# Diagonal of x·yᵀ with softmax: 32 KB runs in 4 MB halves, a last half cut into pieces, and the output moved to ACT's queue

## The chip, the cores and the metric

The kernel runs on one core of one Trainium2 chip. The metric is device time in microseconds (us). The kernel before was run again beside every experiment on the same chip, and its medians there lie between 333.78 and 334.00 us.

Words used throughout: a *dot* is one VectorE instruction that multiplies 128 rows of x by 128 rows of y, 512 numbers each, and sums every row. A *run* is what one packet moves, consecutive bytes of one partition. A *half* is 16 rows per partition, 4 MB of x and 4 MB of y; there are 16, numbered 0 to 15. A load *lands* when its completion is signalled. SP and ACT are the two engines whose queues issue loads here; ACT (ScalarE) also does the exp, and GpSimd the all-reduces over the partitions.

## The reference

```python
B, N, D = 8, 4096, 512            # x, y: float32, standard normal
gram = np.matmul(x, y.transpose(0, 2, 1))
diag = np.diagonal(gram, axis1=1, axis2=2)      # only these 8 x 4096 dots are needed
diag = diag - diag.max(axis=-1, keepdims=True)
exp = np.exp(diag)
return (exp / exp.sum(axis=-1, keepdims=True)).astype(np.float32)
```

The kernel must read 134.2 MB and write 0.13 MB.

## The kernel before

Each of 32 tiles is 8 rows per partition, 2 MB for each input. A batch is four tiles; after the fourth comes its softmax. The parts that matter, cut:

```python
io = ctx.enter_context(tc.tile_pool(name="io", bufs=3))
...
for i in range(n_tiles):                                   # 32 tiles, KR = 8
    x_tile = io.tile([P, KR, D], f32, tag="xt")
    y_tile = io.tile([P, KR, D], f32, tag="yt")
    nc.sync.dma_start(out=x_tile, in_=...)                 # SP queue
    nc.scalar.dma_start(out=y_tile, in_=...)               # ACT queue
    scratch = work.tile([P, D], f32, tag="scratch")        # one per tile
    for k in range(KR):
        nc.vector.scalar_tensor_tensor(
            out=scratch, in0=x_tile[:, k, :], scalar=1.0, in1=y_tile[:, k, :],
            op0=mult, op1=mult, accum_out=diag_sbuf[:, i*KR+k : i*KR+k+1])
    if (i + 1) % tiles_per_batch == 0:
        softmax_batch(b)       # max, all-reduce, exp on ACT, all-reduce, scale, output on SP
```

The order of instructions on each engine is set by the compiler, not by the program text alone.

## Time and profile before

| | us |
|---|---|
| timed, median of 4 runs | 334.00 (333.77 to 334.09) |
| span of the profile | 332.0 |
| last load lands | 321.04 |
| last dot done, maximum begins | 326.93 |
| output issued | 329.31 |

Four lines of the page of the kernel before: busy share of VectorE (DVE) and of the DMA engines in 40 equal slices, in tenths; what they moved; and the group of the dots (count, total busy us, mean ns of one, idle time before them and what ended most of it).

```profile
DVE  0355676543089811898038860588407973089834
...
DMA  8999999999999999999999999999999999999920
GB/s 322 426 438 424 432 423 428 426 427 428 428 436 426 428 422 432 416 426 427 427 432 430 418 432 422 438 377 433 422 431 436 414 431 421 438 393 418 428 127 2
...
L87 DVE SCALAR_TENSOR_TENSOR scratch<-x_tile,y_tile 128x512 f32<-128x512 f32 x256 | 176.9, 691 | 140.0 <-DMA x_tile<-in_x_dram 88.2
```

DMA is busy everywhere but at the ends: loads bound the kernel, and VectorE waits for them. So only three stretches can shrink: the time that the loads themselves take, the dots after the last landing, and the softmax and output after those. The tail, in the timeline of the kernel before (start us, us, engine, line, what, and in brackets the idle time before it and its releaser):

```profile
321.06 0.69 DVE L87 SCALAR_TENSOR_TENSOR scratch<-x_tile,y_tile 128x512 f32<-128x512 f32 x1 [4.96 <-DMA x_tile<-in_x_dram]
321.68 0.08 DVE L87 DVE_READ_ACCUMULATOR scratch<-x_tile,y_tile 128x1 f32 x1
321.80 0.69 DVE L87 SCALAR_TENSOR_TENSOR scratch<-x_tile,y_tile 128x512 f32<-128x512 f32 x1
...
326.93 0.19 DVE L52 TENSOR_REDUCE mxp<-diag_sbuf 128x1 f32<-128x32 f32 x1
...
329.31 0.40 SPq L73 DMA_DIRECT2D out_dram<-result_sbuf  x1
```

Eight dots follow the last landing. They start 0.73 us apart (321.06, 321.80). No load is left by then: the DMA share is 0.00 while they run.

### The profile page before, as it was taken

The page shows a single profiled execution, that of the slowest core. Times are in us where ns is not written, and L with a number is a line of the kernel's source. Part 1 is how long each engine was busy: PE and PEld are TensorE (multiplying, and loading weights), DVE is VectorE, ACT ScalarE, POOL GpSimd, SP SyncE. Part 2 cuts the span into 40 slices and gives each one's busy share as a digit, 9 for nine tenths or more (in the row PEclk, how much of TensorE's full clock was granted, in tenths as well). Part 3 has the DMA queues.
Part 4 walks back from the last instruction along what each step waited for, and adds up shares of the span by engine and source line. Part 5 has one row for each costly group of instructions (what it writes and reads, how often), then busy time and mean ns, then how long its engine had stood idle before and what let it go on. Part 6 is the DMA issues. An engine that isn't in the chain of part 4 may idle for free.

```text
span 332.0 us, 802 instructions
## 1 busy us (share of the span) xinstructions
DVE 183.0 (55%) x544; ACT 4.6 (1%) x17; POOL 6.1 (2%) x20
## 2 busy tenths in 40 slices
DVE  0355676543089811898038860588407973089834
ACT  0000100000000000000000000000000000000000
POOL 0000000000000000000000000000000000000000
DMA  8999999999999999999999999999999999999920
GB/s 322 426 438 424 432 423 428 426 427 428 428 436 426 428 422 432 416 426 427 427 432 430 418 432 422 438 377 433 422 431 436 414 431 421 438 393 418 428 127 2
DMA packets 13446, 134.40 MB, mean 405 GB/s; under 512 B 5248, under 2 KB 5248, under 8 KB 5248
## 3 DMA queue, kind: packets, MB, share of 16 engines
q1 hardware_dynamic: 8832, 67.24, 48.7%
q10 hardware_dynamic: 4608, 67.11, 47.3%
q14 instruction: 6, 0.05, 0.0%
HBM read 134.22 MB, written 0.13 MB: 405 GB/s over the span
## 4 chain that ended last, share of the span: by engine, by line
DMA 69%; DVE 25%; issue 2%; SPq 1%; POOL 1%; ACTq 0%; POOLq 0%; DVEq 0%
DMA x_tile<-in_x_dram 53%; DVE scratch L87 24%; DMA y_tile<-in_y_dram 17%; SPq L73 1%; POOL mx L54 1%; DVE result_sbuf L69 1%; DVE mxp L52 0%; ACTq L82 0%; DVE recip L68 0%; POOLq L124 0%; DVE neg_mx L56 0%; DVEq L69 0%; POOLq L54 0%; SPq L79 0%; DVEq L87 0%
## 5 line engine op out<-in xcount | busy, mean ns | idle before, releaser
L87 DVE SCALAR_TENSOR_TENSOR scratch<-x_tile,y_tile 128x512 f32<-128x512 f32 x256 | 176.9, 691 | 140.0 <-DMA x_tile<-in_x_dram 88.2
L87 DVE DVE_READ_ACCUMULATOR scratch<-x_tile,y_tile 128x1 f32 x256 | 20.8, 81 | 0.0
L54 POOL PARTITION_ALL_REDUCE mx<-mxp x8 | 2.8, 350 | 316.6 <-DVE mxp L52 316.6
L60 ACT ACTIVATE result_sbuf<-diag_sbuf,neg_mx 128x32 f32<-128x32 f32 x8 | 2.6, 321 | 284.5 <-DVE neg_mx L56 284.5
L56 DVE TENSOR_SCALAR neg_mx<-mx 128x1 f32<-128x1 f32 x8 | 1.2, 153 | 4.3 <-POOL mx L54 4.3
L66 POOL PARTITION_ALL_REDUCE ssum<-sump x8 | 3.1, 383 | 5.8 <-ACT result_sbuf L60 5.8
L69 DVE TENSOR_SCALAR result_sbuf<-result_sbuf,recip 128x32 f32<-128x32 f32 x8 | 1.9, 241 | 0.8
L60 ACT ACT_TABLE_LOAD x1 | 1.3, 1283 | 39.1 <-DVE scratch L87 39.1
L68 DVE RECIPROCAL recip<-ssum 128x1 f32<-128x1 f32 x8 | 1.3, 157 | 1.0 <-POOL ssum L66 1.0
L52 DVE TENSOR_REDUCE mxp<-diag_sbuf 128x1 f32<-128x32 f32 x8 | 1.5, 186 | 0.3
L60 ACT ACTIVATION_READ_ACCUMULATOR result_sbuf<-diag_sbuf,neg_mx 128x1 f32 x8 | 1.5, 186 | 0.0
L113 POOL MEMSET const-float32-0.0<- 128x1 f32 x1 | 0.1, 99 | 0.2 <-issue 0.2
L113 POOL MEMSET const-bfloat16-1.0<- 128x1 bf16 x1 | 0.1, 101 | 0.0
L113 POOL MEMSET const-uint8-127<- 128x1 uint8 x1 | 0.1, 101 | 0.0
L113 POOL MEMSET const-float32-1.0<- 128x1 f32 x1 | 0.1, 98 | 0.0
## 6 DMA issues: line engine op xcount, KB each, us to landing
y_tile<-in_y_dram ACTq DMA_DIRECT2D x32, 2048.0 KB, 13.8
x_tile<-in_x_dram SPq DMA_DIRECT2D x32, 2048.0 KB, 23.5
out_dram<-result_sbuf SPq DMA_DIRECT2D x8, 16.0 KB, 17.1
```

Of the source, the lines that this page charges most:

```text
L52: nc.vector.tensor_reduce(out=mxp, in_=db, axis=mybir.AxisListType.X, op=mybir.AluOpType.max)
L54: nc.gpsimd.partition_all_reduce(out_ap=mx, in_ap=mxp, channels=P, reduce_op=bass_isa.ReduceOp.max)
L56: nc.vector.tensor_single_scalar(out=neg_mx, in_=mx, scalar=-1.0, op=mybir.AluOpType.mult)
L60: nc.scalar.activation(out=exp_b, in_=db, func=mybir.ActivationFunctionType.Exp, bias=neg_mx, scale=1.0, accum_out=sump,)
L66: nc.gpsimd.partition_all_reduce(out_ap=ssum, in_ap=sump, channels=P, reduce_op=bass_isa.ReduceOp.add)
L68: nc.vector.reciprocal(out=recip, in_=ssum)
L69: nc.vector.tensor_single_scalar(out=exp_b, in_=exp_b, scalar=recip, op=mybir.AluOpType.mult)
L73: nc.sync.dma_start(out=dst_b, in_=res_b)
L87: nc.vector.scalar_tensor_tensor(out=scratch, in0=x_tile[:, k, :], scalar=1.0, in1=y_tile[:, k, :], op0=mybir.AluOpType.mult, op1=mybir.Al ...
L113: nc = _bacc.Bacc("TRN2", target_bir_lowering=False, num_devices=1)
```

## The change

Its intent: longer runs in HBM (32 KB instead of 16), fewer and larger loads, one straight 128-byte run per partition for the output, and a last half in pieces so that little work is left after the last byte. The diff also moves the output from SP's queue to ACT's and writes each product over x instead of to a scratch tile. The core of the diff, cut and with two comments added; the rest is renaming, and the softmax is the same but for its output.

```diff
-    KR = 8
+    R = N // P          # 32 consecutive rows per partition and batch
+    H = R // 2          # a half: 16 rows, 4 MB for each input
+    xv = x.rearrange("b (p r) d -> b p r d", p=P)
...
+        for n in parts:
+            nc.sync.dma_start(out=xt[:, o : o + n, :], in_=xv[b, :, r0 + o : r0 + o + n, :])
+            nc.scalar.dma_start(out=yt[:, o : o + n, :], in_=yv[b, :, r0 + o : r0 + o + n, :])
...
-                out=scratch,
-                in0=x_tile[:, k, :],
+                out=xt[:, k, :],
+                in0=xt[:, k, :],
...
-        nc.sync.dma_start(out=dst_b, in_=res_b)     # 512 packets of 32 bytes
+        nc.scalar.dma_start(out=ov[b], in_=rb)      # 128 packets of 128 bytes
...
+            parts = [8, 4, 2, 1, 1] if last else [H]
+            xt, yt = load(b, h * H, parts)
+            dots(b, h * H, xt, yt)
+        softmax(b)
```

More of the change, by code (lines that the diff above doesn't have):

```diff
@@ L22 @@
     B, N, D = x.shape
-    assert y.shape == (B, N, D)
-    assert out.shape == (B, N)
     P = nc.NUM_PARTITIONS
-    total = B * N
-    n_chunks = total // P
-    cpb = N // P
-    KR = 8
-    n_tiles = n_chunks // KR
-    tiles_per_batch = N // (P * KR)
-    assert tiles_per_batch * B == n_tiles
-    x_flat = x.flatten_outer_dims()
-    y_flat = y.flatten_outer_dims()
-    out_flat = out.flatten()
+    R = N // P
+    H = R // 2
+    xv = x.rearrange("b (p r) d -> b p r d", p=P)
+    yv = y.rearrange("b (p r) d -> b p r d", p=P)
@@ L41 @@
+    ov = out.rearrange("b (p r) -> b p r", p=P)
     io = ctx.enter_context(tc.tile_pool(name="io", bufs=3))
-    work = ctx.enter_context(tc.tile_pool(name="work", bufs=2))
     persist = ctx.enter_context(tc.tile_pool(name="persist", bufs=1))
     sm = ctx.enter_context(tc.tile_pool(name="sm", bufs=2))
-    diag_sbuf = persist.tile([P, n_chunks], f32)
-    result_sbuf = persist.tile([P, n_chunks], f32)
-    def softmax_batch(b):
-        db = diag_sbuf[:, cpb * b : cpb * (b + 1)]
-        mxp = sm.tile([P, 1], f32, tag="mxp")
-        nc.vector.tensor_reduce(out=mxp, in_=db, axis=mybir.AxisListType.X, op=mybir.AluOpType.max)
-        mx = sm.tile([P, 1], f32, tag="mx")
-        nc.gpsimd.partition_all_reduce(out_ap=mx, in_ap=mxp, channels=P, reduce_op=bass_isa.ReduceOp.max)
-        neg_mx = sm.tile([P, 1], f32, tag="nmx")
-        nc.vector.tensor_single_scalar(out=neg_mx, in_=mx, scalar=-1.0, op=mybir.AluOpType.mult)
-        exp_b = result_sbuf[:, cpb * b : cpb * (b + 1)]
-        sump = sm.tile([P, 1], f32, tag="sump")
-        nc.scalar.activation(
-            out=exp_b, in_=db,
-            func=mybir.ActivationFunctionType.Exp,
-            bias=neg_mx, scale=1.0, accum_out=sump,
-        )
-        ssum = sm.tile([P, 1], f32, tag="ssum")
-        nc.gpsimd.partition_all_reduce(out_ap=ssum, in_ap=sump, channels=P, reduce_op=bass_isa.ReduceOp.add)
-        recip = sm.tile([P, 1], f32, tag="recip")
-        nc.vector.reciprocal(out=recip, in_=ssum)
-        nc.vector.tensor_single_scalar(out=exp_b, in_=exp_b, scalar=recip, op=mybir.AluOpType.mult)
-        res_b = result_sbuf.rearrange("p (i kr) -> p i kr", kr=KR)[:, tiles_per_batch * b : tiles_per_batch * (b + 1), :]
-        dst_b = out_flat[b * N : (b + 1) * N].rearrange("(i p kr) -> p i kr", p=P, kr=KR)
-        nc.sync.dma_start(out=dst_b, in_=res_b)
@@ L75 @@
-    for i in range(n_tiles):
-        r0 = i * P * KR
-        x_tile = io.tile([P, KR, D], f32, tag="xt")
-        y_tile = io.tile([P, KR, D], f32, tag="yt")
-        nc.sync.dma_start(
-            out=x_tile, in_=x_flat[r0 : r0 + P * KR, :].rearrange("(p k) d -> p k d", p=P)
-        )
-        nc.scalar.dma_start(
-            out=y_tile, in_=y_flat[r0 : r0 + P * KR, :].rearrange("(p k) d -> p k d", p=P)
-        )
-        scratch = work.tile([P, D], f32, tag="scratch")
-        for k in range(KR):
+    diag = persist.tile([P, B * R], f32, name="diag")
@@ new lines, with load, dots @@
+    res = persist.tile([P, B * R], f32, name="res")
+    def load(b, r0, parts):
+        xt = io.tile([P, H, D], f32, tag="xt", name="xt")
+        yt = io.tile([P, H, D], f32, tag="yt", name="yt")
+        o = 0
+        for n in parts:
+            nc.sync.dma_start(out=xt[:, o : o + n, :], in_=xv[b, :, r0 + o : r0 + o + n, :])
+            nc.scalar.dma_start(out=yt[:, o : o + n, :], in_=yv[b, :, r0 + o : r0 + o + n, :])
+            o += n
+        return xt, yt
+    def dots(b, r0, xt, yt):
+        for k in range(H):
+            c = b * R + r0 + k
@@ L87, with softmax @@
             nc.vector.scalar_tensor_tensor(
-                out=scratch,
-                in0=x_tile[:, k, :],
+                out=xt[:, k, :],
+                in0=xt[:, k, :],
                 scalar=1.0,
-                in1=y_tile[:, k, :],
+                in1=yt[:, k, :],
                 op0=mybir.AluOpType.mult,
                 op1=mybir.AluOpType.mult,
-                accum_out=diag_sbuf[:, i * KR + k : i * KR + k + 1],
+                accum_out=diag[:, c : c + 1],
             )
-        if (i + 1) % tiles_per_batch == 0:
-            b = (i + 1) // tiles_per_batch - 1
-            softmax_batch(b)
+    def softmax(b):
+        db = diag[:, b * R : (b + 1) * R]
+        rb = res[:, b * R : (b + 1) * R]
+        mxp = sm.tile([P, 1], f32, tag="mxp", name="mxp")
+        nc.vector.tensor_reduce(out=mxp, in_=db, axis=mybir.AxisListType.X, op=mybir.AluOpType.max)
+        mx = sm.tile([P, 1], f32, tag="mx", name="mx")
+        nc.gpsimd.partition_all_reduce(out_ap=mx, in_ap=mxp, channels=P, reduce_op=bass_isa.ReduceOp.max)
+        nmx = sm.tile([P, 1], f32, tag="nmx", name="nmx")
+        nc.vector.tensor_single_scalar(out=nmx, in_=mx, scalar=-1.0, op=mybir.AluOpType.mult)
+        sump = sm.tile([P, 1], f32, tag="sump", name="sump")
+        nc.scalar.activation(
+            out=rb, in_=db, func=mybir.ActivationFunctionType.Exp,
+            bias=nmx, scale=1.0, accum_out=sump,
+        )
+        ssum = sm.tile([P, 1], f32, tag="ssum", name="ssum")
+        nc.gpsimd.partition_all_reduce(out_ap=ssum, in_ap=sump, channels=P, reduce_op=bass_isa.ReduceOp.add)
+        rc = sm.tile([P, 1], f32, tag="rc", name="rc")
+        nc.vector.reciprocal(out=rc, in_=ssum)
+        nc.vector.tensor_single_scalar(out=rb, in_=rb, scalar=rc, op=mybir.AluOpType.mult)
+        nc.scalar.dma_start(out=ov[b], in_=rb)
@@ L102 @@
+    for b in range(B):
+        for h in range(2):
+            last = b == B - 1 and h == 1
+            parts = [8, 4, 2, 1, 1] if last else [H]
+            xt, yt = load(b, h * H, parts)
+            dots(b, h * H, xt, yt)
+        softmax(b)
 _INS = ['x', 'y']
```

## The prediction

> **What bounds the kernel now.** Loads. The page's DMA row is at 9 tenths in every slice but the first and the last two, and moves some 428 GB/s; VectorE is busy 55%. In the trace's packet records nearly every 16 KB packet takes 611 ns on its engine, so 8192 of them on 16 engines are 312.8 us; they actually run from 1.7 to 319.6 us. The Trainium skill ("DMA: Bandwidth & Descriptors", Measured) gives 425 GB/s for a single core's 16 MB transfer, the same rate; so the bytes are at their ceiling, and the change moves the same bytes. Only what stands before the first packet (1.7 us), the roughly 5 us lost between packets, and the tail can shrink.
>
> **The tail (timeline).** The last x tile lands at 321.04; eight dot products of 0.733 us each follow (5.87 us), VectorE ends them at 326.9, and maximum, two all-reduces, exp, sum, scaling and the output DMA take 5.1 us more to 332.0. The timed median is 1.9 us over this span.
>
> **What the change does.**
> - Bigger descriptors (32 KB): 8 KB instruction packets took 307 ns and 16 KB 611, so some 3 ns are fixed; halving their number is worth 0.5 us or so.
> - Outputs: 32-byte packets fall from 4096 to 1024 of 128 bytes. They took 7 to 9 ns each; estimate 1 to 1.5 us saved over 16 engines.
> - Dropped scratch (product in place): the same instruction, nothing.
> - Output on ACT instead of SP: SP no longer stands behind the result (80 us of such waits on SP's queue). But DMA was never starved by them, because y filled in; it only removes the skew (x was up to 15 us behind y). x and y should now land together. Three 4 MB buffers keep over 8 us queued at all times (period 19.6 us, VectorE 11.7 us per half), so nothing starves.
> - First half lands at about 23 us instead of 13: harmless, VectorE catches up.
> - Tail: the last row pair is one 0.73 us dot product, but VectorE is then not idle. The half before it, 16 dots (11.7 us), starts 19.6 us before the last byte; 32 dots need 23.5 us. So VectorE ends about 3.9 us after the last landing (plus 0.3 for batch 6's reciprocal and scaling), not 0.73. Gain over 5.87: about 1.7 us, not 5.
>
> Sum: 332.0 - 1.7 (tail) - 1.3 (DMA) = 329.0 span; timed about 331.
>
> **Prediction: 331.0 us**, 80% between 328.0 and 334.5. Faster by over 2%: 0.07; within: 0.89; slower: 0.04.
>
> **What would show it.** The DMA row still near 428 GB/s; last load landing near 319.5; at that time VectorE still working on the 8-row or 4-row piece, without a gap from the start of the second-last half (16 dots) to the end; no idle time before the 1-row pieces' dots; x and y landing within about 1 us of each other throughout; span minus last landing about 9 us, before 11.
>
> **What would make it wrong.**
> - The instruction order is the compiler's. There seem to be 8 DMA semaphores in rotation (each load waits for the DMA eight before). If ACT gets the five y pieces before batch 6's exp, exp waits for the 8-row piece, the reciprocal for exp, and VectorE stalls: 5 to 11 us slower.
> - 32 KB runs at a 64 KB pitch could be read more slowly from HBM. The skill (same page, "Latency and other measured facts") shows such losses at far larger pitches of 512 KB and up; no run here shows it.
> - If packet stalls vanish (1 us at 216 and at 296 us of this trace), 327 is possible.
> - Skew left at the end lengthens the tail, since VectorE then gets both halves closer together.

## More of the kernel before

Most experiments ran on one chip; e10, e11 and e12 ran on another, where the kernel before took 333.88 us against 333.78 and 333.81. Differences between runs of separate sessions are therefore good to some 0.2 us.

The *lag* is the time by which the last of the DMA engines ends a load after the middle one.

## The result, and the profile after

The change took **331.92 us** (331.86 to 332.06, 4 runs) against 334.00: ratio 0.9939, 95% interval 0.9925 to 0.9953. Ratios here are the mean time of one kernel's fast runs over that of the other's fast runs of the same rounds, so not quite the ratio of the medians. The verdict is "same" at the 2% mark; a small gain is clear of noise.

| us | before | after | difference |
|---|---|---|---|
| last load lands | 321.04 | 318.36 | -2.7 |
| from there to the start of the maximum | 5.9 | 7.0 | +1.1 |
| from there to the end of the span | 5.1 | 4.7 | -0.4 |
| span | 332.0 | 330.0 | -2.0 |

The loads gained more than the whole kernel did, and the tail, which the pieces were to shorten, got *longer*. The same lines of the page of the change:

```profile
DVE  0029093470920561910878290660388465191995
...
DMA  8999999999999999999999999999999999999900
GB/s 318 445 445 445 409 426 433 445 445 409 423 441 445 441 405 429 439 445 429 413 431 445 445 418 417 439 441 445 409 427 441 441 433 410 443 417 423 396 37 3
...
L51 DVE SCALAR_TENSOR_TENSOR xt<-xt,yt 128x512 f32<-128x512 f32 x256 | 158.1, 687 | 151.8 <-DMA yt<-in_y_dram 151.8
```

Two things stand out. All of VectorE's large waits (151.8 us) are now for y, none for x. And the 256 dots keep VectorE busy for 158 us instead of 177, though one still takes about 690 ns: they overlap more. The tail in the change's timeline:

```profile
305.56 6.70 ACTq L44 DMA_DIRECT2D yt<-in_y_dram  x4
305.63 0.69 DVE L51 SCALAR_TENSOR_TENSOR xt<-xt,yt 128x512 f32<-128x512 f32 x1 [5.82 <-DMA yt<-in_y_dram]
306.25 0.69 DVE L51 SCALAR_TENSOR_TENSOR xt<-xt,yt 128x512 f32<-128x512 f32 x1
...
324.62 0.69 DVE L51 SCALAR_TENSOR_TENSOR xt<-xt,yt 128x512 f32<-128x512 f32 x1
325.35 0.19 DVE L65 TENSOR_REDUCE mxp<-diag 128x1 f32<-128x32 f32 x1
...
327.75 0.35 ACTq L80 DMA_DIRECT2D out_dram<-res  x1
```

Half 14 became complete only at 305.5, when its y landed; its x had landed at 288.7. From then on VectorE does 32 dots without a pause, 0.613 us apart (305.63, 306.25), which is 19.6 us, while the last byte lands only 12.8 us after half 14. VectorE therefore ends 7.0 us after the last landing, working off a backlog. The size of the last piece no longer matters.

Why y trails shows on ACT's own queue. In the change's timeline of ACT (ACTq is its sequencer, which issues the loads), around the first softmax:

```profile
52.84 0.32 ACT L71 ACTIVATE res<-diag,nmx 128x32 f32<-128x32 f32 x1 [49.45 <-DVE nmx L69]
52.85 0.34 ACTq L44 DMA_DIRECT2D yt<-in_y_dram  x1
53.07 0.19 ACT L71 ACTIVATION_READ_ACCUMULATOR res<-diag,nmx 128x1 f32 x1
63.94 0.35 ACTq L80 DMA_DIRECT2D out_dram<-res  x1
64.33 0.44 ACTq L44 DMA_DIRECT2D yt<-in_y_dram  x1
```

The y load issued at 52.85 had its buffer free since 32.5, and the x load of the same half went out on SP at 32.54. It stood behind the exp, which needed the dots of the next half. The y load at 64.33 stood behind the output; its x partner went out at 51.98. The trace has this order, exp, y, output, y, for each of the batches 0 to 5.

The trace's packet records showed a third thing. Each load ends on each of 16 DMA engines with a 4-byte packet, so one can see when each engine finished. (The records do not name the engine; that it is one and the same is read from there being one late packet per load.) In the last y load of the change, the middle engine was done at 314.19 and the last one at 317.91: **one DMA engine ran 3.7 us behind the rest**, and the landing is set by the last. In the last x load of the kernel before that lag was 1.8 us.

### The profile page after: what moved, and what is told of

Read it like the earlier page. It is cut to its first block, busy times and chain, and to the rows that moved or that the text cites. A ratio compares the mean times of both kernels' runs of the same rounds, so it can differ in the third digit from the quotient of the medians.

```text
span 330.0 us, 732 instructions
## 1 busy us (share of the span) xinstructions
DVE 163.9 (50%) x544; ACT 4.6 (1%) x17; POOL 6.1 (2%) x20
## 4 chain that ended last, share of the span: by engine, by line
DMA 72%; DVE 24%; issue 2%; POOL 1%; ACTq 0%; POOLq 0%; DVEq 0%; ACT 0%
DMA yt<-in_y_dram 72%; DVE xt L51 23%; POOL mx L67 1%; DVE mxp L65 0%; DVE nmx L69 0%; ACTq L44 0%; DVE res L79 0%; POOLq L114 0%; POOL ssum L76 0%; DVE rc L78 0%; ACTq L80 0%; ACT res L71 0%; DVEq L51 0%; POOLq L67 0%; DVEq L79 0%
## 5 line engine op out<-in xcount | busy, mean ns | idle before, releaser
L51 DVE SCALAR_TENSOR_TENSOR xt<-xt,yt 128x512 f32<-128x512 f32 x256 | 158.1, 687 | 151.8 <-DMA yt<-in_y_dram 151.8
L51 DVE DVE_READ_ACCUMULATOR xt<-xt,yt 128x1 f32 x256 | 21.1, 82 | 0.0
L71 ACT ACTIVATE res<-diag,nmx 128x32 f32<-128x32 f32 x8 | 2.6, 321 | 320.0 <-DVE nmx L69 320.0
L78 DVE RECIPROCAL rc<-ssum 128x1 f32<-128x1 f32 x8 | 1.3, 163 | 6.7 <-POOL ssum L76 6.7
L69 DVE TENSOR_SCALAR nmx<-mx 128x1 f32<-128x1 f32 x8 | 1.2, 154 | 4.3 <-POOL mx L67 4.3
L79 DVE TENSOR_SCALAR res<-res,rc 128x32 f32<-128x32 f32 x8 | 1.9, 241 | 0.7
L65 DVE TENSOR_REDUCE mxp<-diag 128x1 f32<-128x32 f32 x8 | 1.5, 186 | 0.3
L71 ACT ACTIVATION_READ_ACCUMULATOR res<-diag,nmx 128x1 f32 x8 | 1.5, 186 | 0.0
```

The costliest lines, as they stand in the source:

```text
L51: nc.vector.scalar_tensor_tensor(out=xt[:, k, :], in0=xt[:, k, :], scalar=1.0, in1=yt[:, k, :], op0=mybir.AluOpType.mult, op1=mybir.AluOpT ...
L65: nc.vector.tensor_reduce(out=mxp, in_=db, axis=mybir.AxisListType.X, op=mybir.AluOpType.max)
L69: nc.vector.tensor_single_scalar(out=nmx, in_=mx, scalar=-1.0, op=mybir.AluOpType.mult)
L71: nc.scalar.activation(out=rb, in_=db, func=mybir.ActivationFunctionType.Exp, bias=nmx, scale=1.0, accum_out=sump,)
L78: nc.vector.reciprocal(out=rc, in_=ssum)
L79: nc.vector.tensor_single_scalar(out=rb, in_=rb, scalar=rc, op=mybir.AluOpType.mult)
```

## The experiments

Eleven kernels ran; all gave the reference's result. Theory A: the skew between x and y, made by ACT's order, lengthens the tail. Rivals: the queue count, or the pieces themselves. Further theories concern the in-place product, the run length, the outputs and the lagging engine. All numbers, the decisive columns from timeline and landings (blank: not used). At the 2% mark e1 and e6 are faster than the kernel before, e8 and e10 unclear, and all others the same:

| run | timed us | ratio to before | half 14 complete | last load lands | maximum begins |
|---|---|---|---|---|---|
| the change | 331.92 | 0.9939 | 305.5 | 318.4 | 325.4 |
| e1 y on SP | 325.50 | 0.9752 | 298.4 | 318.2 | 319.1 |
| e5 e1 with self-wait | 328.31 | 0.9834 | 298.4 | 318.3 | 321.9 |
| e9 y early | 332.31 | 0.9951 | 306.0 | 318.3 | 326.0 |
| e10 in step, two queues | 327.57 | 0.9813 | 298.7 | 318.4 | 319.2 |
| e4 no pieces | 334.88 | 1.0032 | 308.4 | 318.1 | 328.2 |
| e12 e1 without pieces | 334.25 | 1.0012 | 298.4 | 317.8 | 327.8 |
| e6 e1, few instructions | 322.98 | 0.9671 | 295.7 | 315.7 | 316.5 |
| e11 e1, more instructions | 329.36 | 0.9869 | 301.3 | 322.1 | 322.9 |
| e7 e1 with 16 KB runs | 328.15 | 0.9827 | | 320.7 | |
| e8 e1 with 32-byte outputs | 327.20 | 0.9803 | | 318.2 | 319.1 |
| e3 before, in place | 332.88 | 0.9970 | | 320.8 | 325.8 |

### e1: y on SP

```diff
-            nc.scalar.dma_start(out=yt[:, o : o + n, :], ...)
+            nc.sync.dma_start(out=yt[:, o : o + n, :], ...)
```

> The change with the y loads moved from the ACT queue to the SP queue, nothing else. Theory A (y's loads stand behind exp and the output on ACT, so y trails x by up to 20 us, the last two halves become complete only 12.8 us apart, and VectorE's 32 dot products of 0.613 us = 19.6 us end 7.0 us after the last landing): x and y of a half now land within 1 us of each other, the second-last half is complete about 19 us before the last landing, VectorE ends 1 to 2 us after the last landing, time 326.5 to 328 us against 331.9 for the change. Rival B (the tail is set by the pieces and the landing of the last one, skew does not matter): time within 1 us of 331.9. Rival C (one queue feeds the DMA engines less well than two): DMA rate below 428 GB/s, last landing later than 320.

Measured: 325.50 us, 6.4 us under the change (difference of the medians) and 1.0 below the range expected. The last landing hardly moved (318.23), so the loads run no worse from one queue. Half 14 was complete 19.9 us before it, and VectorE all but kept up. The end of e1's timeline:

```profile
317.05 0.69 DVE L51 SCALAR_TENSOR_TENSOR xt<-xt,yt 128x512 f32<-128x512 f32 x1
317.67 0.08 DVE L51 DVE_READ_ACCUMULATOR xt<-xt,yt 128x1 f32 x1
318.33 0.69 DVE L51 SCALAR_TENSOR_TENSOR xt<-xt,yt 128x512 f32<-128x512 f32 x1 [0.58 <-DMA yt<-in_y_dram]
318.94 0.08 DVE L51 DVE_READ_ACCUMULATOR xt<-xt,yt 128x1 f32 x1
319.06 0.19 DVE L65 TENSOR_REDUCE mxp<-diag 128x1 f32<-128x32 f32 x1
```

Now the last dot waits 0.58 us for the last row: the tail is one dot long, as the change had intended. Theory A holds and rivals B and C fall; whether a single queue as such was the cause is left to e9 and e10. One slip in the expectation: with a single queue x and y of a half do not land within 1 us of each other but take turns about 10 us apart; what matters is that whole halves become complete evenly.

### e9 and e10: in step on two queues

e9 leaves y on ACT and moves the loads up in the program.

```diff
+    tiles = {j: load_half(j) for j in range(3)}
+    for j in range(2 * B):
+        ...
+        dots(b, h * H, xt, yt)
+        if j + 3 < 2 * B:
+            tiles[j + 3] = load_half(j + 3)
+        if h == 1:
+            softmax(b)
```

> The change with y left on the ACT queue, but each half's loads are written in the program right after the dots that free its buffer, ahead of that batch's softmax, so that on ACT most y loads no longer stand behind exp and the output. It tells skew from queue. Theory A (skew between x and y is what lengthened the tail): x and y land within 2 us of each other, second-last half complete 18 us or more before the last landing, VectorE ends 1 to 2 us after it, time 325 to 327. Rival (a single queue as such made e1_y_on_sp fast): time stays near 331.9.

Measured: 332.31 us, and the skew was still there (half 14 complete at 306.0): the edit missed its aim, so this run tells nothing between skew and queue. In its trace the first batch's output went out on ACT only at 102.8, since VectorE reached that batch's reciprocal late; the y load behind it left at 103.2, its x partner at 91.7. After that, x and y of a half are issued within 2.1 us of each other, up to half 14, and yet from half 6 to half 14 y lands 19 to 31 us after x. The likely reading: x, with less waiting in its queue, lands first, and then has to wait for buffers that only y can free. The delay, once there, did not heal; no run separates the first late load from the 2 us that y loses behind every later output. (The semaphore that the expectation of e10 speaks of told of VectorE's result: VectorE scales it at 102.51.)

e10 is e9 with the outputs on the GpSimd queue.

```diff
-        nc.scalar.dma_start(out=ov[b], in_=rb)
+        nc.gpsimd.dma_start(out=ov[b], in_=rb)
```

> e9_y_early missed its aim: on ACT an output waiting for its semaphore still stood in front of a y load early on, y fell behind, and the lag never healed (second-last half complete at 306.0, last landing 318.3, as in the change). Here the outputs go out on the GpSimd queue as well, so that ACT holds only y loads, each ahead of the exp that becomes ready at the same time. x on SP and y on ACT, two queues. Theory A (skew, not the number of queues): x and y of a half land within 2 us of each other, second-last half complete 18 us or more before the last landing, VectorE ends 1 to 2 us after it, time 325 to 327. Rival (one queue as such made e1_y_on_sp fast): 331 to 332.

Measured: half 14 complete at 298.7, last landing 318.4, maximum at 319.2: all within 0.5 us of e1, with two queues. In e10's timeline the last dot waits for the last row, as in e1:

```profile
318.48 0.69 DVE L51 SCALAR_TENSOR_TENSOR xt<-xt,yt 128x512 f32<-128x512 f32 x1 [0.38 <-DMA yt<-in_y_dram]
319.10 0.08 DVE L51 DVE_READ_ACCUMULATOR xt<-xt,yt 128x1 f32 x1
319.22 0.19 DVE L65 TENSOR_REDUCE mxp<-diag 128x1 f32<-128x32 f32 x1
```

So skew was the cause and not the queue count. The timed 327.57 is 0.6 over the expected range and 2.1 over e1. Of this 1.2 us is the output: in e10 it is issued at 321.80 and lands at 324.04 (2.2 us); in e1, from ACT, at 321.45 and 322.87 (1.4 us). The other 0.9 us falls after that landing or outside the profile's span, and no run explains it.

### e4 and e12: what the pieces are worth

```diff
-            parts = [8, 4, 2, 1, 1] if last else [H]
+            parts = [H]
```

> The change without its pieces: the last half is one load of 16 rows for each input. Theory A: 16 dots (9.8 us) must follow the last landing, which gains nothing else: VectorE ends 9.8 us after the last landing instead of 7.0, time 334 to 335.5 us. Rival (VectorE's backlog already sets the end, pieces give nothing): 331.9. It also tells whether the DMA engine that ends 3.7 us after the others in the change does so because of the small pieces (then the spread at the end falls below 1 us here) or drags behind all along (then it stays at 3 us or more).

> As e1_y_on_sp, without pieces: the last half is one load each for x and y. Theory A: with x and y in step the pieces are worth what they were meant to be worth: VectorE ends 16 dots = 9.8 us after the last landing instead of 0.8, time 334 to 334.7, so 9 us more, where taking the pieces out of the change itself cost 3.0 us (e4_no_pieces). Rival (pieces are worth the same 3 us whatever the skew): 328.5.

Measured: taking the pieces out of the change costs 3.0 us (334.88 against 331.92); taking them out of e1 costs 8.8 us (334.25 against 325.50). Busy time by stretches (us from start to end, its length, VectorE busy and instructions, ACT, GpSimd, clock, DMA share, GB/s), for e4 and then e12, from the completion of half 14 to the last landing, to the maximum, to the end:

```profile
308.41:318.11 9.70, 9.61 (x31) 0.00 (x0) 0.00 (x0) 1.00 0.53 225
318.11:328.20 10.09, 10.08 (x34) 0.00 (x0) 0.00 (x0) 1.00 0.00 0
328.20:332.90 4.70, 0.74 (x4) 0.41 (x2) 0.73 (x2) 1.00 0.02 3
```

```profile
298.42:317.83 19.41, 9.89 (x32) 0.00 (x0) 0.00 (x0) 1.00 0.77 330
317.83:327.85 10.02, 9.89 (x33) 0.00 (x0) 0.00 (x0) 1.00 0.00 0
327.85:332.50 4.65, 0.74 (x4) 0.41 (x2) 0.73 (x2) 1.00 0.02 4
```

Both leave 10 us after the last landing. In e12 VectorE idles half of the 19.4 us before it, time that pieces can use; in e4 it is busy throughout. With x and y in step the pieces are worth 8.8 us, and the skew took most of it. The lag of one DMA engine was 4.0 us or more in both, so it does not come from the pieces.

### e3 and e5: the product in place

```diff
-                out=scratch,
+                out=x_tile[:, k, :],          # e3, in the kernel before
```

> The kernel before, with only the product written in place instead of to the scratch tile; instruction order unchanged. Theory A (self-wait gone): pitch 0.613 us, the last tile's 8 dots take 4.9 instead of 5.87 us, time 1.0 us less, about 333.0. Rival (place of the product is free): 334.0.

```diff
-                out=xt[:, k, :],
+                out=xt[:, 0, :],              # e5, in e1: every dot writes over the last one's product
```

> As e1_y_on_sp (same instruction order on SP, ACT and VectorE), but every dot product of a half writes its product over row 0 of the x tile, so that each waits for the one before, as the one scratch tile made it do in the kernel before. Results stay right. Theory A (the in-place write took away a wait of VectorE on itself: 0.733 us from one dot to the next before, 0.613 after): pitch back to 0.73 us, 32 dots 23.5 us, VectorE ends 4 to 5 us after the last landing, time 3 to 4 us over e1_y_on_sp, so 330 to 331.5. Rival (the place of the product costs nothing, as the prediction said): pitch 0.61, same time as e1_y_on_sp.

The semaphores that the traces keep with each instruction show the difference: with one scratch (and in e5), every dot after a tile's first waits for a semaphore that the dot before it raises; with a place of its own for each product (e3, e1, the change), none does. In e3's timeline the last tile's dots start 0.61 us apart:

```profile
320.80 0.69 DVE L86 SCALAR_TENSOR_TENSOR x_tile<-x_tile,y_tile 128x512 f32<-128x512 f32 x1 [5.56 <-DMA x_tile<-in_x_dram]
321.41 0.08 DVE L86 DVE_READ_ACCUMULATOR x_tile<-x_tile,y_tile 128x1 f32 x1
321.41 0.68 DVE L86 SCALAR_TENSOR_TENSOR x_tile<-x_tile,y_tile 128x512 f32<-128x512 f32 x1
```

e3 came to 332.88, 0.9 us under the kernel before beside it (333.78), as 8 times 0.12 us says. e5's dots start 0.73 us apart again:

```profile
318.22 0.69 DVE L51 SCALAR_TENSOR_TENSOR xt<-xt,yt 128x512 f32<-128x512 f32 x1
318.84 0.08 DVE L51 DVE_READ_ACCUMULATOR xt<-xt,yt 128x1 f32 x1
318.96 0.69 DVE L51 SCALAR_TENSOR_TENSOR xt<-xt,yt 128x512 f32<-128x512 f32 x1
```

It took 2.8 us more than e1 (3 to 4 were expected), with the same order on SP, ACT and VectorE. The wait is real and only costs where VectorE is last: some 1 us in the kernel before, and more the more dots are left at the end. e5 is also what the prediction had in mind (x and y in step, dots 0.733 us apart): the maximum begins 3.6 us after the last landing, where it had said 3.9 plus 0.3.

### e7: run length

```diff
-            parts = [8, 4, 2, 1, 1] if last else [H]
+            parts = [8, 4, 2, 1, 1] if last else [8, 8]
```

> As e1_y_on_sp, but every half is loaded as two pieces of 8 rows, so that runs are 16 KB again, as in the kernel before. Theory E (a run costs some 9 ns beyond its bytes, since 16 KB packets took 611 ns and 32 KB packets 1213): twice the packets, 0.6 ns per KB, so the packets take 2.1 to 2.3 us more per engine, last landing about 320.4 instead of 318.2, time 327.7. Prediction's size (3 ns a run): 0.5 us, 326.0. Rival (run length does not matter): 325.5.

Measured: 328.15 us, 2.65 over e1; last landing 320.7 against 318.2. In the packet records a 16 KB packet takes 611 ns in the kernel before and 613 in e7, a 32 KB packet 1213 in e1, so two short ones cost 9 to 13 ns more than one long one. e7 has 3840 such pairs, which on 16 engines make 2.2 to 3.1 us. Theory E holds; e7 also doubles the number of loads, and only these packet times tie its cost to the runs.

That e7 moves the landing nearly as far as the change did (2.5 and 2.7 us) is in part chance. Summed over all packets, an engine was busy 318.9 us in the kernel before and 314.1 in the change. Of these 4.8 us, 1.4 are output packets (2.3 to 0.8), and 1.7 are stalls, load packets that took over 0.1 us longer than most (1.9 to 0.2 after the first 5 us; in the kernel before mainly at 139, 218 and 297 us). The rest is longer runs and fewer loads. The middle engine ended its last load 4.0 us sooner (318.15 to 314.19), the last one only 2.0 (319.92 to 317.91).

### e8: small output packets

```diff
-        nc.scalar.dma_start(out=ov[b], in_=rb)
+        for g in range(4):
+            nc.scalar.dma_start(out=ov[b][:, 8 * g : 8 * g + 8], in_=rb[:, 8 * g : 8 * g + 8])
```

> As e1_y_on_sp, but each output goes out as four DMAs of 8 columns, so again as 512 packets of 32 bytes a batch instead of 128 of 128 bytes. Theory F (small packets take DMA engine time from the loads, 7 to 9 ns each): 3072 packets more, 1.5 us of engine time spread over 16 engines, less their data; last landing 1 to 1.5 us later, time 326.5 to 327. Rival (they vanish between the loads): 325.5, at most 0.3 us from the last output.

Measured: 327.20 us, 1.7 over e1 and 0.2 over the expected range, and for another reason than the one expected. The last load landed at 318.22, as in e1 (318.23). The time went into the last output: its four DMAs are issued one after the other and the last lands at 324.30 instead of 322.87. Fifteen engines did finish the last load later (the middle one at 315.90 instead of 314.16) but the lagging one did not (317.85 and 317.78), and it decides. So the small packets do take time from the loads, 1.7 us on most engines, but here it hid behind the lag; Theory F falls as far as the end of the loads goes. Why the lagging engine was spared stays open.

### e6 and e11: the lagging engine

In e1's packet records one engine ends the last load 3.6 us after the middle one. Four 8 KB packets of the instruction queue run during e1's loads, at 47, 125, 185 and 263 us, and beside each there is a 32 KB packet that takes 1.87 us instead of 1.21. The lag steps up after each of them: 0.33 us before the first, then 0.90, 1.86, 2.83 and 3.84. e6 gives VectorE 2 instructions a half in place of 16 dots, but for the last batch (names in the two cuts are shortened):

```diff
+        nc.vector.tensor_tensor(out=xt, in0=xt, in1=yt, op=mult)
+        nc.vector.tensor_reduce(out=diag[:, c : c + H], in_=xt, axis=X, op=add)
```

> As e1_y_on_sp (325.5 us), but the halves of batches 0 to 6 take two VectorE instructions (one product of 128x8192 in place, one sum over 512) instead of 16 dot products; the last batch keeps its dots and pieces. In the traces so far one DMA engine ends 3.6 us after the other fifteen, and the lag grows by about 1 us after each 8 KB packet of the instruction queue (four of them, near 48, 125, 186 and 263 us in e1_y_on_sp). Theory D (the engine that also fetches instructions drags behind and sets the last landing): with a tenth of the instructions the four fetches and the long packets beside them go away, the lag at the end falls below 1 us, the last landing comes 2.5 to 3.5 us sooner (about 315), time 322 to 323.5. Rival (this engine is slow whatever is fetched): lag stays over 3 us, last landing 318.2, time 325.5. VectorE gets busier (estimate 8192 products and 8192 sums at the pace of a 512-wide dot, some 17 to 20 us per half against 19.5 us of loading): if it is over 19.5 it becomes the bound, and the time rises; then only the lag in the packets decides.

e11 adds instructions:

```diff
+            if b < B - 1:
+                for e in (2 * c, 2 * c + 1):
+                    nc.vector.tensor_copy(out=junk[:, e : e + 1], in_=yt[:, k, e % 2 : e % 2 + 1])
```

> As e1_y_on_sp, with two useless one-element copies on VectorE after every dot product of batches 0 to 6 (448 in all; results stay right). In e1_y_on_sp four 8 KB packets of the instruction queue ran during the loads, one for some 64 dots, so a dot takes about 128 bytes and a copy, of one instruction, perhaps half that. Theory D (instruction fetches delay one DMA engine by about 1 us each): seven or eight fetches instead of four, the last engine ends 6 to 8 us after the others instead of 3.6, last landing 3 us later (about 321), time 328 to 329.5. Rival (the lag has nothing to do with fetches): lag 3.6, time 325.5. VectorE has room: 16 dots with their copies take some 13 us of the 19.5 us between halves.

| run | instruction packets during the loads | lag of the last DMA engine, us | last load lands |
|---|---|---|---|
| e6 | 1 | 0.94 | 315.69 |
| e1 | 4 | 3.62 | 318.23 |
| e11 | 8 | 7.01 | 322.12 |

About 0.9 us of lag for each packet, over a range of eight. Not every packet adds to it: e7 has a fifth, at 289.8 us, beside a 16 KB packet that took 1.03 us instead of 0.61, and its lag stood at 3.94 us before and 3.98 after. Lines of the page of e6 (queue, kind, packets, MB, share; then VectorE's groups), and after them the queue line of e11:

```profile
span 321.2 us, 312 instructions
## 1 busy us (share of the span) xinstructions
DVE 268.5 (84%) x124; ACT 4.6 (1%) x17; POOL 6.1 (2%) x20
...
q14 instruction: 1, 0.01, 0.0%
...
L50 DVE TENSOR_TENSOR xt<-xt,yt 128x8192 f32<-128x8192 f32 x14 | 121.6, 8689 | 36.3 <-DMA yt<-in_y_dram 36.3
L51 DVE TENSOR_REDUCE diag<-xt 128x16 f32<-128x8192 f32 x14 | 121.6, 8686 | 0.5
```

```profile
q14 instruction: 8, 0.07, 0.0%
```

Theory D holds: fetching instructions delays one DMA engine, and because every load is spread over all 16, that engine sets the last landing. e6 makes VectorE *busier* (84% instead of 51%) and the kernel *faster*, 322.98 us: 3.3% under the kernel before, 2.7% under the change. It is the best version found.

One thing stays open here. The kernel before had five such packets before its last load ended and yet a lag of only 1.8 us at the end; its lag rises and falls along the run. e8 bears on it: with four packets and outputs in 32-byte packets again it ends with 1.9 us, since its other engines end later. So the small outputs seem to be part of it. No run tested the rest.

## Why the prediction was right or wrong

The time, 331.9, lay inside the range and within 1 us of the 331.0 named; the forecast "within 2%" held. The sum was right by luck, because two wrong terms nearly cancelled.

- *"the bytes are at their ceiling"*: right in the main, since the DMA row stayed full. The Trainium skill ("DMA: Bandwidth & Descriptors", Measured) gives 425 GB/s for 16 MB (issued from GpSimd); by the stretches view the kernel before moved 429 GB/s between 20 and 100 us and the change 432.
- *DMA, -1.3 us*: it was -2.7. The step that failed is the size of *"Bigger descriptors (32 KB) ... worth 0.5 us or so"*, which took 3 ns a packet from 8 KB instruction packets. e7 measured 2.65 us. The outputs, down for *"1 to 1.5 us"*, took 1.4 us less of each engine's time, but in e8 putting them back left the last landing where it was. *"If packet stalls vanish"* came true, another 1.7 us of each engine's time. The lag of the fetching engine, not in the prediction at all, held back part of the gain (1.8 to 3.7 us).
- *Tail, -1.7 us*: it was +1.1. The step that failed is *"x and y should now land together"*, drawn from moving the output off SP. The move put y behind exp and output on ACT; e1 and e10 bring x and y into step and gain 6.4 and 4.4 us. The prediction's last warning, skew left at the end, named just this.
- *"Dropped scratch ... the same instruction, nothing"*: wrong. The instruction is the same but the wait before it went: 0.12 us a dot (e3, e5). An estimate from these runs: at 0.733 us a dot the change's 32 dots would have ended some 10.7 us after the last landing (23.5 less 12.8), 3.7 us later than they did.
- *"VectorE is then not idle ... about 3.9 us after the last landing"*: the mechanism, a backlog of 32 dots against the time between two landings, was right and is what ended the kernel; its inputs were 12.8 us and 0.613 us a dot, not 19.6 and 0.733. e5 has the assumed inputs and shows 3.6 us.
- *After the dots*: nothing was forecast; it fell by 0.4 us. The output, now with long runs and from ACT, lands 1.4 us after its issue instead of 1.8.
- *"If ACT gets the five y pieces before batch 6's exp ... VectorE stalls"*: it did not happen in the change. It did in e9 and e10, where that exp ran late, but VectorE had 21 other dots to do before the reciprocal, and e10 shows no stall.

## What to carry to other kernels

Before moving a load to another engine's queue, read what else that engine does in order: a load behind an exp or an output inherits their waits, and two streams that are needed together are only as good as the later one. A tail is a race between work left and bytes left, so compare the last two landings with the work they release; cutting the last piece helps less when the engine is behind already (3.0 us here against 8.8). When every DMA engine carries a share of each load, look at when the last one finishes, and count instructions: here fewer VectorE instructions with more VectorE work were the faster kernel.

## What the Trainium skill lacked or had wrong

- "Runtime: NRT & Kernel Launch", Instruction fetch mechanics, has instructions refilled in 16 KiB blocks at a cost "mostly hidden". Here the refills show as 8 KB packets, about one for 64 dots, and left one DMA engine about 0.9 us further behind each (lags of 0.94, 3.62 and 7.01 us with 1, 4 and 8 packets). In a kernel bound by loads it was not hidden: 2.5 us between e1 and e6.
- "VectorE: DVE Perf Modes", The DRAIN you can't avoid, measured that a semaphore between copies "costs nothing extra", and has no figure for its remark that an instruction that is not held starts earlier. For dots with an accumulator, waiting for the previous one cost 0.12 us each (0.733 against 0.613 us from start to start; e3, e5).
- "DMA: Bandwidth & Descriptors" says nothing on runs above a few KB in this detail: 16 KB packets took 611 to 613 ns and 32 KB packets 1213; loads in 16 KB runs cost 2.65 us of 328 (e7).
- The same page, Issuing engines are not separate DMA queues, was borne out: last landing 318.2 with SP alone (e1), 318.4 with SP and ACT (e10). No page warns that a lag between two queues need not heal (e9: y landed 19 to 31 us behind x up to half 14, after one load issued 11.5 us late and every other one some 2 us late).
- No page that was read sets the time from issue to landing of one small output from ACT beside that from GpSimd: for the same 16 KB it was 1.4 us (e1) and 2.2 us (e10).
